# Norm factors of the memory rows: from the start of the attention to the second projection chunk

## The chip, the cores and the metric

The kernel runs on one core of a Trainium2 chip. The metric is the device time of one execution in microseconds (us). The engines are TensorE (PE, matmuls and transposes), VectorE (DVE), ScalarE (ACT), GpSimd (POOL) and SyncE (SP, which here only issues DMAs).

## The reference

One decoder layer on x of 1024 rows by 1024 columns, in float32, with 256 rows of memory. What matters here, cut:

```python
def rmsnorm(x, g):
    y = x * lax.rsqrt(jnp.mean(x * x, axis=-1, keepdims=True) + EPS)
    return y * g

def token_mixer(hn, ...):
    proj = hn @ w_in                      # split into q_a, k_a, v_a, q_i, k_i, w_i, q_b, k_b, v_b
    ...                                   # norms and rope of the heads
    out_a = dsa_attention(q_a, k_a, v_a, q_i, k_i, w_i)   # top-256 keys per query by index scores
    out_b = diff_attention(q_b, k_b, v_b, lam)            # softmax(q1 k1) - lam softmax(q2 k2), times v
    return jnp.concatenate([out_a, rms_normalize(out_b) * (1.0 - lambda_init)], axis=-1) @ w_out

def cross_attention(hn, memn, w_xq, w_xk, w_xv, w_xo, g_xq, g_xk):
    q = rmsnorm((hn @ w_xq).reshape(B, S, 4, 256), g_xq)
    k = rmsnorm((memn @ w_xk).reshape(B, 256, 4, 256), g_xk)
    v = (memn @ w_xv).reshape(B, 256, 4, 256)
    ...

h = h + token_mixer(rmsnorm(h, g_mix), ...)
h = h + cross_attention(rmsnorm(h, g_xattn), rmsnorm(mem, g_mem), ...)
h = h + conv_glu(rmsnorm(h, g_ffn), ...)
```

The change concerns `rmsnorm(mem, g_mem)`: its factor per memory row, rsqrt(mean of squares + EPS).

## The kernel before

The work runs in stages. In the first (0 to about 60 us) x is read, its rows' squares are summed, and chunk 0 of the input projection (index queries, keys and the like) is computed. Tiles of 128x1024 float32 for this lie in a ring of five buffers, pool `early`, tag "xr": raw rows of x (`xraw`) and then four `c1x` tiles, each with the results of two blocks of 128 rows. The pool is closed in chunk 1, at t == 2, and its room goes to the masks and scores of the top-k search.

Chunks 1 to 4 of the projection follow (60 to 270 us). Each has eight row tiles t: `proj_mm(c, t)` makes 24 matmuls on PE (L308 to L310, products of high and low halves), and ACT evacuates the result with the row factor (X, L646). In chunk 1 DVE, POOL, ACT and PE also work on the c1x tiles (`c1_post`, `c1_tr`: rope, splits L457/L458, key transposes L494 with their copies L496) and on index scores. In chunks 2 to 4 the threshold of the top-k search is bisected (`topk_iter`): counts by ACT (L553) for one group of row tiles and by DVE (L565) for another, with the small updates on DVE (L555, L557, L570, L571).

The differential attention starts at about 270 us, in steps s from -4. For unit u, a head and a block of 128 queries, there are: the load of the q tile `qt` (`b_load_q`, L731, SP's queue), its split on POOL into high and low part `hl` (`b_split`, L738 and L739), the transposes on PE (`b_qt`, L746, copied by ACT L748 into `qbs`), scores on PE (`b_s`, L766/L767), their masking and scaling on DVE (`e`, L774) and exponentials on ACT (L776), the difference of the two softmaxes on DVE (`b_comb`, L784 to L786), transposes of it (`b_t`, L691) and the product with v (`b_av`, L797). Keys of a head are loaded as `ktok` (L705), scaled on POOL into `kdup` (L721), transposed (L723) and split (`kb`, L725 on ACT and L726 on DVE). `b_load_v` (L712) loads `vb`.

The projections of the memory (`mem_mm`, L885, into `acc`; weights `wp` loaded at L247) are spread over the steps of this attention as units. ACT evacuates a unit with the memory rows' factors `rm` (`mem_evac`, L889); for keys a head norm follows (L894 ACT, L896, L107 to L116 and L900 DVE, with the gain product `gkq`). `mem_prep` stands ahead of the steps: it loads the two memory tiles `mtok` of 128x1024 (L873, buffers that the attention's `e` tiles use too), sums their squares on ACT (L875) into `ssm`, loads the two gains `gx` (L877, L878) and multiplies them on POOL (`gkq`, L879). At s == -2 `rstd` makes `rm` from `ssm`: ten small rows on POOL (L107, L108, L118 to L127); on DVE the same helper makes nine (L107, L108, L110 to L116).

The engines' queues are ordered by a scheduler that simulates a timeline, with the calls above as its program order. So an edit at one place can change the order of rows elsewhere.

Of the kernel before, what the change touches and what calls it, by code (L numbers as in the profile page):

```python
# [18 lines left out]
P = 128  # L19
# [25 lines left out]
def hybrid_layer(ctx, tc, I, out):  # L45
# [15 lines left out]
    def nm(s):  # L61
        cnt[0] += 1
        return f"{s}_{cnt[0]}"
# [575 lines left out]
    def proj_mm(c, t):  # L639
        pages = W.get(("in", c), 8)  # L640
        p = accp()
        s = slice(t * P, (t + 1) * P)
        for k in range(KT):
            mm3(p, xh[k][:, s], xl[k][:, s], pages[k][:, 0, :], pages[k][:, 1, :], k == 0, k == KT - 1)
        X = rt("X", [P, 512], F32, "X")
        last["act"] = act.activation(X, p, AF.Copy, scale=rx[:, t:t + 1])  # L646
        return X
# [164 lines left out]
    store = None  # L812
    idxq = [lambda t=t, h=h: idx_head(t, h) for t in range(2, NT) for h in range(4)]
    mb, sc = {}, {}
    for t in range(NT):
        X = proj_mm(1, t)
        if t == 2:
            early_st.close()
            scp_st, scp = open_pool("scp")
            for i in range(2, NT):  # L820
                mb[i] = scp.tile([P, P * (i + 1)], BF, name=f"mb{i}")
                sc[i] = scp.tile([P, P * (i + 1)], F32, name=f"sc{i}")
        if t == 7:
            W.free(8)
        W.pump(2 if t == 3 else 1)
        for a in steps[t]:
            if a == "i":
                idxq.pop(0)()
            else:
                (c1_post if a[0] == "p" else c1_tr)(int(a[1]))  # L830
        if store:
            store()
        store = proj_post(1, t, X)
# [24 lines left out]
    def etile(name):  # L858
        return obp.tile([P, T], F32, name=nm(name), tag="e", bufs=4)
# [7 lines left out]
    def mem_prep():  # L867
        pages = W.get("memT", 2)
        for j in range(KT):
            mstat[j] = pages[j // 4].bitcast(F32)[:, j % 4 // 2, (j % 2) * 256:(j % 2) * 256 + 256]  # L870
        for t in range(2):
            xt = etile("mtok")
            sp.dma_start(xt, I["mem"][t * P:(t + 1) * P, :])  # L873
            jk = rt("t2", [P, T], BF, "jk")
            act.activation(jk, xt, AF.Square, accum_out=ssm[:, t:t + 1])  # L875
        gx = rt("t2", [P, 2, 256], F32, "gx")
        sp.dma_start(gx[:, 0, :], rows(I["g_xq"]))  # L877
        sp.dma_start(gx[:, 1, :], rows(I["g_xk"]))  # L878
        pool.tensor_tensor(gkq, gx[:, 0, :], gx[:, 1, :], op=OP.mult)  # L879
# [70 lines left out]
    for s in range(-4, NB):  # L950
        h, i = b_units[max(s, 0)]
        m = s % NT

        def ok(u):
            return 0 <= u < NB
        if s % 4 == 0:
            if s >= 0:
                b_acc[s // 4] = accp()
        if s + 5 >= 2 and ok(s + 5):
            b_load_q(s + 5)  # L960
        if s >= 0 and h < 3 and m == 1:
            b_load_k(h + 1)
            b_load_v(h + 1)
        if ok(s + 4):
            b_split(s + 4)
        if s == -2:
            rstd(pool, rm, ssm, 2, 1.0 / D)
        if ok(s + 3):
            b_qt(s + 3)
        if ok(s):  # L970
            b_t(s)
        if ok(s + 2):
            b_s(s + 2)
        mem_step(MB)
        if ok(s + 1):
            b_comb(s + 1)
        if s >= 0 and h < 3 and 2 <= m <= 5:
            b_k(h + 1, (m - 2) // 2, 4 * (m % 2))
        if ok(s):
            b_av(s)  # L980
            W.pump(1)
            tick(0.8 + 0.85 * (i + 1))
# [753 lines left out]
```

## Time and profile before

| | us |
|---|---|
| median of 3 runs | 1676.73 (1675.79 to 1676.85) |
| profiled execution | 1677.18 |
| its span, first to last instruction | 1675.4 |
| PE busy / DVE / ACT / POOL | 1572.9 / 1222.3 / 804.1 / 641.2 |

Times in the trace count from the start of the span. A row of a timeline gives the start, the time and the operation with its output and input tiles (numbers left out); in brackets stands how long the engine had been idle before it, and what ended that. A row that stands for several instructions ends with their count.

### The profile page before, as it was taken

What the parts mean: (1) busy time and instruction counts of PE and PEld (TensorE: products, weight loads), DVE (VectorE), ACT (ScalarE), POOL (GpSimd) and SP (SyncE); (2) the same over time, 40 slices, a digit from 0 to 9 for tenths busy, and PEclk for the clock granted to TensorE, in tenths of its full rate; (3) what the DMA queues carried; (4) which work ended last, traced back from release to release, by engine and by line L of the source; (5) the groups of instructions that cost most, each with busy time, mean ns of one, the idle gap of its engine ahead of it and who ended that gap; (6) DMA issues with size and microseconds to landing.
All of it is one profiled execution on the core that took longest, in us unless ns stands there. A gap on an engine that the chain in (4) does not pass through costs nothing.

```text
span 1675.4 us, 22263 instructions
## 1 busy us (share of the span) xinstructions
PE 1572.9 (94%) x7596; PEld 1273.4 (76%) x7596; DVE 1222.3 (73%) x2356; ACT 804.1 (48%) x1696; POOL 641.2 (38%) x888
## 2 busy tenths in 40 slices
PE   8899987878888999999999997999999999999999
PEld 7788765666657888977777785888888777788887
DVE  5736998886778876346555369998899999865554
ACT  6545575576777445527443175432333333343432
POOL 2736656223361122031101013556666666651121
PEclk9999998989999999999999998999999999999999
DMA  8321236212120132153203021455555555799812
GB/s 283 99 83 47 77 126 212 75 51 74 49 66 27 51 101 77 45 175 115 101 1 113 26 89 63 163 170 188 177 176 178 183 187 184 253 357 379 307 51 76
DMA packets 112162, 220.06 MB, mean 131 GB/s; under 512 B 18480, under 2 KB 38448, under 8 KB 112048
## 3 DMA queue, kind: packets, MB, share of 16 engines
q1 hardware_dynamic: 91072, 148.37, 26.5%
q0 software_dynamic: 18384, 61.36, 10.3%
q10 hardware_dynamic: 2592, 8.91, 1.4%
q8 instruction: 60, 0.98, 0.2%
q14 instruction: 54, 0.44, 0.1%
HBM read 160.92 MB, written 57.67 MB: 130 GB/s over the span
## 4 chain that ended last, share of the span: by engine, by line
PE 57%; DVE 23%; DMA 7%; ACT 6%; issue 4%; POOL 3%; SPq 0%; ACTq 0%; DVEq 0%; POOLq 0%
PE acc L308 9%; PE acc L310 9%; PE acc L309 9%; PE big L309 3%; PE big L310 3%; PE big L308 3%; DVE wp L204 3%; PE acc L1036 2%; DVE jk L565 2%; PE trp L308 2%; PE trp L310 2%; PE trp L309 2%; PE trp L691 2%; DMA raw<-in_w_ffn_in_dram 2%; PE acc L885 2%
## 5 line engine op out<-in xcount | busy, mean ns | idle before, releaser
L204 DVE TENSOR_TENSOR wp<-raw,wp 128x512 fp32r<-128x512 f32 (+1 forms) x184 | 183.4, 1006 | 28.3 <-ACT wp L201 17.2
L201 ACT CAST wp<-raw 128x512 fp32r<-128x512 f32 (+1 forms) x184 | 108.4, 615 | 176.6 <-DVE raw L227 113.6
L1600 DVE TENSOR_TENSOR wp<-fo,wp 128x1024 fp32r<-128x1024 f32 x77 | 104.2, 1370 | 75.3 <-ACT wp L1599 71.6
L1549 POOL TENSOR_TENSOR fs<-fs,fs 128x512 f32<-128x512 f32 x88 | 127.6, 1450 | 63.4 <-DMA fs<-u_d 49.0
L1599 ACT CAST wp<-fo 128x1024 fp32r<-128x1024 f32 x77 | 79.8, 1049 | 107.7 <-PE big L310 46.1
L308 PE MATMUL acc<-wp,xh 128*128 128x512 f32 (+1 forms) x272 | 110.1, 407 | 10.0 <-ACT X L646 10.0
L310 PE MATMUL acc<-wp,xl 128*128 128x512 f32 (+1 forms) x272 | 109.5, 403 | 0.0
L309 PE MATMUL acc<-wp,xh 128*128 128x512 f32 (+1 forms) x272 | 109.2, 403 | 0.0
L553 ACT ACTIVATE mb<-sc,cand 128x384 bf16<-128x384 f32 (+1 forms) x96 | 75.4, 786 | 39.6 <-DVE cand L557 35.8
L203 POOL TENSOR_SCALAR wp<-raw 128x512 fp32r<-128x512 f32 (+1 forms) x36 | 24.9, 698 | 177.0 <-DVE rst L110 63.5
L682 ACT COPY pt<-trp 128x512 f32<-128x512 f32 (+3 forms) x144 | 66.3, 476 | 41.2 <-PE trp L691 40.6
L1036 PEld LDWEIGHTS acc<-va_t,pt 128*128 128x128 f32 x576 | 75.1, 196 | 9.6 <-ACT pt L682 7.6
L1036 PE MATMUL acc<-va_t,pt 128*128 128x65 f32 x576 | 77.8, 274 | 4.0 <-ACT pt L682 3.8
L1646 POOL TENSOR_TENSOR hr<-hr,r 128x512 f32<-128x512 f32 x16 | 26.8, 1686 | 115.6 <-DMA fo<-ws_d 58.4
L308 PEld LDWEIGHTS acc<-wp,xh 128*128 128x128 f32 x272 | 52.7, 194 | 23.5 <-ACT X L646 12.2
L1018 DVE CUSTOM_DVE_ANT_0 ea<-big,mb,ra 128x384 f32<-128x384 f32 (+5 forms) x48 | 45.4, 946 | 27.5 <-PE trp L691 24.4
L1497 ACT ACTIVATE fc<-fc 128x1024 f32<-128x1024 f32 x22 | 23.4, 1062 | 84.8 <-DVE fc L1496 84.8
L204 POOL TENSOR_TENSOR wp<-raw,wp 128x512 fp32r<-128x512 f32 x36 | 47.5, 1336 | 42.1 <-ACT wp L201 41.8
L774 DVE CUSTOM_DVE_ANT_0 e<-big,tri,rqk 128x1024 f32<-128x1024 f32 (+7 forms) x64 | 50.4, 812 | 16.9 <-PE big L767 14.6
L1494 ACT ACTIVATE fc<-fa,cw 128x1024 f32<-128x1024 f32 x22 | 27.4, 1245 | 71.5 <-DVE fa L1453 71.5
L1019 ACT ACTIVATE ea<-ea,sta 128x128 f32<-128x128 f32 (+7 forms) x64 | 49.5, 777 | 24.9 <-DVE sta L1018 23.0
L310 PEld LDWEIGHTS acc<-wp,xl 128*128 128x128 f32 x272 | 52.4, 193 | 11.5
(422 smaller groups left out, 5133.3 us busy)
## 6 DMA issues: line engine op xcount, KB each, us to landing
raw<-in_w_ffn_in_dram SPq DMA_DIRECT2D x44, 512.0 KB, 4.0
fs<-in_w_ffn_out_dram POOLq DMA_DIRECT2D x44, 256.0 KB, 3.5
ws_d<-fs POOLq DMA_DIRECT2D x44, 256.0 KB, 2.3
fs<-u_d POOLq DMA_DIRECT2D x44, 256.0 KB, 3.8
us_d<-fs POOLq DMA_DIRECT2D x44, 256.0 KB, 3.5
fo<-us_d SPq DMA_DIRECT2D x44, 256.0 KB, 5.4
fo<-ws_d SPq DMA_DIRECT2D x44, 256.0 KB, 5.4
u_d<-fg POOLq DMA_DIRECT2D x21, 512.0 KB, 3.7
```

The source lines that it names most:

```text
L201: act.copy(pg[:, 0, :n], src)
L204: (dve if el == "d" else pool).tensor_tensor(pg[:, 1, :n], src, pg[:, 0, :n].bitcast(F32), op=OP.subtract)
L308: pe.matmul(o, lhsT=lh, rhs=rh, start=start, stop=False)
L309: pe.matmul(o, lhsT=lh, rhs=rl, start=False, stop=False)
L310: pe.matmul(o, lhsT=ll, rhs=rh, start=False, stop=stop)
L553: act.activation(mb[i], sc[i], AF.Sign, bias=cf[:, j:j + 1], scale=-1.0, accum_out=cnt[:, j:j + 1])
L682: act.copy(dst, src)
L774: dve.tensor_tensor_reduce(e[:, :n], Ss[c][:, :n], tri[:, T - n:], rqk[h // 2][:, i, 2 * (h % 2) + c:2 * (h % 2) + c + 1], 3.0e38, OP.add, ...
L1036: pe.matmul(acc[:, hh * 65:hh * 65 + 65], lhsT=pt, rhs=va_t[:, kt, :], start=kt == 0, stop=kt == i)
L1549: pool.tensor_tensor(o, p, q, op=op)
L1599: act.copy(hi, raw)
L1600: dve.tensor_tensor(lo, raw, hi.bitcast(F32), op=OP.subtract)
```

## The change

A new function `mem_norm(t)` loads memory tile t into the ring of the first stage (tag "xr", the five buffers of 128x1024), sums its squares on ACT and, for the second tile, makes `rm` with the helper `rstd` on DVE. It is called for t = 0 and 1 right behind `proj_mm(1, t)`. The loop over the two tiles in `mem_prep` and the call of `rstd` on POOL at s == -2 are taken out.

```diff
--- before.py
+++ after.py
@@ -812,8 +812,20 @@
     store = None
     idxq = [lambda t=t, h=h: idx_head(t, h) for t in range(2, NT) for h in range(4)]
     mb, sc = {}, {}
+
+    def mem_norm(t):
+
+        xt = early.tile([P, T], F32, name=nm("mtok"), tag="xr", bufs=5)
+        sp.dma_start(xt, I["mem"][t * P:(t + 1) * P, :])
+        jk = rt("t2", [P, T], BF, "jk")
+        act.activation(jk, xt, AF.Square, accum_out=ssm[:, t:t + 1])
+        if t == 1:
+            rstd(dve, rm, ssm, 2, 1.0 / D)
+
     for t in range(NT):
         X = proj_mm(1, t)
+        if t < 2:
+            mem_norm(t)
         if t == 2:
             early_st.close()
             scp_st, scp = open_pool("scp")
@@ -868,11 +880,6 @@
         pages = W.get("memT", 2)
         for j in range(KT):
             mstat[j] = pages[j // 4].bitcast(F32)[:, j % 4 // 2, (j % 2) * 256:(j % 2) * 256 + 256]
-        for t in range(2):
-            xt = etile("mtok")
-            sp.dma_start(xt, I["mem"][t * P:(t + 1) * P, :])
-            jk = rt("t2", [P, T], BF, "jk")
-            act.activation(jk, xt, AF.Square, accum_out=ssm[:, t:t + 1])
         gx = rt("t2", [P, 2, 256], F32, "gx")
         sp.dma_start(gx[:, 0, :], rows(I["g_xq"]))
         sp.dma_start(gx[:, 1, :], rows(I["g_xk"]))
@@ -963,8 +970,6 @@
             b_load_v(h + 1)
         if ok(s + 4):
             b_split(s + 4)
-        if s == -2:
-            rstd(pool, rm, ssm, 2, 1.0 / D)
         if ok(s + 3):
             b_qt(s + 3)
         if ok(s):
```

On POOL, at the start of the attention, this stood before (`rst` and `rm` are the norm factors, `hl` with `qt` the split of a q tile, `kdup` scaled keys, `gkq` the gain product):

```order
L122 TENSOR_TENSOR rst_2762<-rst_2762 128x2
L123 TENSOR_TENSOR rst_2762<-rst_2762 128x2
L738 TENSOR_SCALAR hl_2759<-qt_2744 128x2x64
L124 TENSOR_SCALAR rst_2762<-rst_2762 128x2
L739 TENSOR_TENSOR hl_2759<-qt_2744,hl_2759 128x2x64
L125 TENSOR_TENSOR rst_2762<-rst_2762 128x2
L126 TENSOR_SCALAR rst_2762<-rst_2762 128x2
L127 TENSOR_TENSOR rm<-rst_2762 128x2
L738 TENSOR_SCALAR hl_2801<-qt_2757 128x2x64
L739 TENSOR_TENSOR hl_2801<-qt_2757,hl_2801 128x2x64
L721 TENSOR_TENSOR kdup_3016<-ktok_2894,rqk_76 128x4x64 x2
L879 TENSOR_TENSOR gkq<-gx_2737 128x256
```

And this stands there now, right behind the same splits of the first two q tiles:

```order
L886 TENSOR_TENSOR gkq<-gx_2747 128x256
L738 TENSOR_SCALAR hl_2769<-qt_2754 128x2x64
L721 TENSOR_TENSOR kdup_3013<-ktok_2891,rqk_76 128x4x64 x2
L739 TENSOR_TENSOR hl_2769<-qt_2754,hl_2769 128x2x64
L738 TENSOR_SCALAR hl_2798<-qt_2767 128x2x64
L721 TENSOR_TENSOR kdup_3081<-ktok_2892,rqk_76 128x4x64 x2
L721 TENSOR_TENSOR kdup_3138<-ktok_2891,rqk_76 128x4x64 x2
L739 TENSOR_TENSOR hl_2798<-qt_2767,hl_2798 128x2x64
```

The norm factors are gone; the gain product has come ahead of the third q tile's split, and two rows of scaled keys between its halves L738 and L739.

On SP's queue at the same place, the loads before (`wp` weights of the memory projection, `vb` values, `qa_d` a store of normed queries of the other attention):

```order
L247 DMA wp_3157<-in_w_xv_dram 128x2x512
L712 DMA vb_2727<-vb_d 128x8x128
L873 DMA mtok_2729<-in_mem_dram 128x1024
L873 DMA mtok_2733<-in_mem_dram 128x1024
L712 DMA vb_2902<-vb_d 128x8x128
L247 DMA wp_3211<-in_w_xv_dram 128x2x512
L675 DMA qa_d<-X_2599 128x512
L731 DMA qt_2744<-qk_d_91 128x128
L705 DMA ktok_2894<-qk_d_91 128x4x128
L675 DMA qa_d<-X_2654 128x512
L731 DMA qt_2757<-qk_d_91 128x128
```

And the loads now:

```order
L247 DMA wp_3154<-in_w_xv_dram 128x2x512
L712 DMA vb_2745<-vb_d 128x8x128
L712 DMA vb_2899<-vb_d 128x8x128
L247 DMA wp_3208<-in_w_xv_dram 128x2x512
L675 DMA qa_d<-X_2617 128x512
L884 DMA gx_2747<-in_g_xq_dram 128x256
L885 DMA gx_2747<-in_g_xk_dram 128x256
L731 DMA qt_2754<-qk_d_91 128x128
L705 DMA ktok_2891<-qk_d_91 128x4x128
L675 DMA qa_d<-X_2672 128x512
L731 DMA qt_2767<-qk_d_91 128x128
```

Two loads of 128x1024 are gone, and the two gain loads have moved from behind the keys to the place ahead of the first q tile.

On DVE in chunk 1 of the projection the rows of the norm factors (`rst`, nine rows, the last into `rm`) now stand between the rope of c1x tiles; the rows without `rst` and `rm` stood there before in the same order:

```order
L452 TENSOR_TENSOR c1x_548<-c1x_548,tb_785 128x64
L107 TENSOR_SCALAR rst_849<-ssm 128x2
L481 TENSOR_TENSOR c1x_548<-c1x_548,t_128_788 128x384
L108 TENSOR_SCALAR rst_849<-rst_849 128x2
L483 TENSOR_SCALAR kk_123_764<-c1x_548,rka 128x128
L452 TENSOR_TENSOR c1x_553<-c1x_553,csn 128x320
L110 SCALAR_TENSOR_TENSOR rst_849<-rst_849 128x2
L497 TENSOR_TENSOR ka_102<-trp_668,ka_101 128x128
L452 TENSOR_TENSOR c1x_553<-c1x_553,tb_867 128x64
L111 TENSOR_TENSOR rst_849<-rst_849 128x2
L481 TENSOR_TENSOR c1x_553<-c1x_553,t_143_870 128x384
L112 SCALAR_TENSOR_TENSOR rst_849<-rst_849 128x2
```

So the first row of `rst`, which waits for ACT's second square, stands ahead of one c1x tile's L481 and of its key scaling L483.

## Rows read from the trace of the kernel before

**Rows 1.** The page's first part: busy time, share of the span, instructions.

```profile
PE 1572.9 (94%) x7596; PEld 1273.4 (76%) x7596; DVE 1222.3 (73%) x2356; ACT 804.1 (48%) x1696; POOL 641.2 (38%) x888
```

**Rows 2.** Windows: us, busy time and instructions by engine, granted PE clock, DMA share, GB/s.

```profile
70.00:190.00 120.00, 120.00 (x548) 97.94 (x547) 74.24 (x146) 61.34 (x122) 68.87 (x104) 1.00 0.23 72
280.00:290.00 10.00, 3.78 (x14) 2.63 (x12) 6.08 (x16) 5.81 (x13) 2.38 (x7) 0.71 1.07 339
310.00:320.00 10.00, 6.04 (x39) 5.14 (x38) 10.00 (x24) 6.54 (x16) 2.41 (x4) 0.92 0.26 84
```

**Rows 3.** Waits, 262 to 312 us: who waited for whom, us in total, times, longest.

```profile
POOL rst L107 <- ACT jk L875: 7.7, 1, 7.7
PE trp L746 <- POOL hl L739: 7.6, 1, 7.6
```

**Rows 4.** Chain of work that ended last, 250 to 312 us: start, us, what.

```profile
273.93 9.68 DMA mtok<-in_mem_dram
```

**Rows 5.** Timeline of SP's DMA queue: start, us of the issue, line, transfer.

```profile
282.06 0.38 SPq L731 DMA_DIRECT2D qt<-qk_d  x1
```

**Rows 6.** DMA issues at 282.0 to 282.4 us: size, us from issue to landing.

```profile
qt<-qk_d SPq DMA_DIRECT2D x1, 64.0 KB, 7.3
```

**Rows 7.** Timeline of POOL, 269 to 302 us: start, us, operation, tiles, idle time before.

```profile
287.10 0.19 POOL L107 TENSOR_SCALAR rst<-ssm 128x2 f32<-128x2 f32 x1 [7.70 <-ACT jk L875]
...
290.21 0.30 POOL L738 TENSOR_SCALAR hl<-qt 128x128 fp32r<-128x128 f32 x1
...
290.90 0.46 POOL L739 TENSOR_TENSOR hl<-qt,hl 128x128 fp32r<-128x128 f32 x1
...
292.83 1.20 POOL L721 TENSOR_TENSOR kdup<-ktok,rqk 128x256 f32<-128x256 f32 x2
293.99 0.73 POOL L879 TENSOR_TENSOR gkq<-gx 128x256 f32<-128x256 f32 x1
```

**Rows 8.** Timeline of DVE, 269 to 302 us.

```profile
284.87 0.48 DVE L774 CUSTOM_DVE_ANT_0 e<-big,tri,rqk 128x256 f32<-128x256 f32 x1 [0.72 <-ACT jk L875]
...
288.17 0.17 DVE L784 RECIPROCAL st<-st 128x2 f32<-128x2 f32 x1 [2.40 <-ACT e L776]
...
293.62 0.69 DVE L896 TENSOR_REDUCE ss<-sq 128x2 f32<-128x512 f32 x1 [0.72 <-ACT sq L894]
...
295.30 0.56 DVE L111 TENSOR_TENSOR rst<-rst 128x2 f32<-128x2 f32 x1
...
297.53 1.14 DVE L774 CUSTOM_DVE_ANT_0 e<-big,tri,rqk 128x896 f32<-128x896 f32 x1
```

**Rows 9.** Timeline of PE, 269 to 320 us.

```profile
291.42 0.69 PE L746 MATMUL trp<-ident,hl 128*128 128x128 f32 x2 [7.64 <-POOL hl L739]
...
294.12 0.78 PE L766 MATMUL big<-kb,qbs 128*128 128x512 f32 x1
...
312.56 0.50 PE L766 MATMUL big<-kb,qbs 128*128 128x512 f32 x1 [2.03 <-DVE st L774]
...
317.90 0.33 PE L691 MATMUL trp<-ident,e 128*128 128x128 f32 x1 [1.93 <-DVE kb L726]
```

**Rows 10.** Timeline of ACT, 269 to 302 us.

```profile
283.69 1.06 ACT L875 ACTIVATE jk<-mtok 128x1024 bf16<-128x1024 f32 x1 [3.17 <-DMA mtok<-in_mem_dram]
```

**Rows 11.** Timeline of ACT, 44 to 80 us.

```profile
61.20 0.41 ACT L457 CAST hl<-c1x 128x256 fp32r<-128x256 f32 x1 [2.76 <-DVE hl L458]
...
65.38 0.27 ACT L496 CAST ka<-trp 128x128 fp32r<-128x128 f32 x1 [2.99 <-PE trp L494]
...
73.01 0.69 ACT L646 ACTIVATE X<-acc,rx 128x512 f32<-128x512 f32 x1 [2.00 <-PE acc L310]
```

**Rows 12.** DMA issues at 50.7 to 50.9 us.

```profile
raw<-in_w_in_dram SPq DMA_DIRECT2D x1, 512.0 KB, 4.7
```

**Rows 13.** Waits, 190 to 242 us.

```profile
PE acc L308 <- ACT X L646: 10.0, 5, 3.9
```

**Rows 14.** The page's costliest groups: xcount | busy, mean ns | idle before.

```profile
L553 ACT ACTIVATE mb<-sc,cand 128x384 bf16<-128x384 f32 (+1 forms) x96 | 75.4, 786 | 39.6 <-DVE cand L557 35.8
```

## The prediction

> **What bounds the kernel now.** I read the page first. TensorE (PE) works for 1572.9 us, 94% of a span of 1675.4 us [rows 1], so a change off PE can only win where PE stands still. The windows by stage say where that is: from 70 to 190 us PE is busy all the time [rows 2], while in 280 to 290 us it works 3.78 us of 10 and VectorE (DVE) 6.08. That second place is the start of the differential attention, which the change touches.
>
> The list of waits of 262 to 312 us says who waits there [rows 3]: PE waits 7.6 us, once, for POOL's row L739 (the split of a q tile); POOL itself waits 7.7 us, once, for ScalarE's (ACT's) square L875 of a memory tile. The chain of waits goes one step further back, in one row: 9.68 us of "DMA mtok", the tile's load [rows 4]. So the program looks as if it stood still for memory rows that nobody needs yet, with the q tile queued behind the norm factors on POOL.
>
> Three more views are needed before that 7.6 us may be believed. First the DMA issues: the q tile `qt` that L738/L739 split is issued on SP's queue at 282.06 [rows 5] and takes 7.3 us to land [rows 6]. It lands at 282.06 + 7.3 = 289.4 us. POOL's wait ends at 287.10, and L738 runs at 290.21 [rows 7]: without any norm factors, POOL could have started the split only 0.8 us earlier. The load takes 7.3 us because the DMA engines are full: share 1.07 and 339 GB/s in 280 to 290 us [rows 2].
>
> Second, DVE. It waits 2.40 us for ACT's exponentials at 288.17, 0.72 us for an ACT square at 284.87 and 0.72 us for an ACT square of the memory keys at 293.62 [rows 8]. The next score rows `e` (step 2) start on DVE at 297.53 only, although PE's matmuls for them began at 294.12 [rows 8, 9].
>
> Third, what ends last behind this. In 310 to 320 us DVE is busy for the whole 10 us and PE for 6.04 [rows 2]; PE waits there 2.03 us for DVE's statistics (L774) and 1.93 us for DVE's `kb` (L726) [rows 9]. So what the start of the attention is worth is set by how early DVE gets through its own rows, and PE can give up at most these waits plus what it gains itself.
>
> **The change, part by part.** All times below are from the one profiled execution.
>
> *Removed: two memory loads.* 2 x 512 KB = 1.05 MB leave the queue ahead of the q tile. At 339 GB/s this is 1.05 MB / 339 GB/s = 3.1 us for all that lands behind them. The order of SP's queue shows that the two gain loads `gx` (2 x 128 KB = 0.26 MB, 0.8 us at the same rate) now stand ahead of the q tile, where before they stood behind it. So the q tile should land at 289.4 - 3.1 + 0.8 = 287.1 us, and `ktok` right behind it, whose 256 KB take 0.8 us at that rate, at 287.9 us.
>
> *Removed: ten POOL rows of norm factors.* On POOL now stand ahead of L739: `gkq` (0.73 us), L738 (0.30) and two `kdup` rows (1.20 together) [rows 7]. From 286.9 us, when `gx` should be there: gkq to 287.6, L738 to 287.9, kdup to 289.1, L739 (0.46) to about 289.6. PE's transposes of this tile began at 291.42 [rows 9]; they should begin at about 289.7. **PE's own gain is 1.7 us**, not 7.6, since most of the wait goes from POOL's square to POOL's data.
>
> *Removed: two ACT squares from the place.* Each is 1.06 us [rows 10] and the reading of its sum behind it; together over 2.1 us that stood among the exponentials. They are why DVE waited 2.40 and 0.72 us [rows 8]. The evacuation of the first memory unit (L889) no longer waits for `rm`, so the key norm on DVE (L896, L107 to L116) can run while DVE had nothing to do; the order shows these rows ahead of and between the first score rows. **DVE's gain is at most 0.72 + 2.40 + 0.72 = 3.84 us.** Step 2's score matmuls stood 2.7 us behind the transposes, since the cast between them waited behind L889 on ACT; without that they start at about 290.8 rather than 294.12, 3.3 us earlier, and so don't hold DVE back from taking its 3.84.
>
> Which of 1.7 and 3.84 counts? PE's two waits for DVE at 312.56 and 317.90 [rows 9] are the next thing that ends last, so it is nearer to DVE's. I go seven tenths of the way from the one to the other: 1.7 + 0.7 x 2.14 = 3.2 us, with 1.7 and 3.84 as the bounds.
>
> *Added in the first stage: two loads, two squares, nine DVE rows.* The squares come on ACT behind rows at which ACT stood idle (2.99 us before 65.38, 2.00 us before 73.01 [rows 11]): two of 1.06 us fit. The first load stands ahead of one weight load that took 4.7 us [rows 12]; 512 KB more at 339 GB/s makes that 1.5 us later. ACT, which casts these weights, then had 2.76 us idle before 61.20 [rows 11], which takes it in. The second load takes the slot of a c1x tile and can start only when DVE and ACT have read that; I put this at 66.5 us, and at 4.7 us it lands by 71.2, when ACT has just become free (73.01 - 2.00 = 71.0). The nine DVE rows cost at most 0.56 us each by a row of the same helper on as few columns [rows 8], so 5.0 us; DVE works 74.24 of 120 us in 70 to 190 us while PE is full [rows 2]. The cover for all this is PE's projection matmuls. If it is gone, because the second load comes later than 71.8 us, the X evacuation at 73.01 and the transposes behind DVE come late by as much: up to 2 us. I take 0.
>
> *Moved: the rows between 195 and 270 us.* The scheduler orders each queue anew. At five places an X evacuation (L646) now stands behind one more pair of top-k counts (L553) on ACT. PE waits there for just these evacuations: 10.0 us in 5 waits [rows 13]. But DVE, which releases these counts, has up to 2 us less work ahead of them in the new order (and the nine norm rows lie earlier, in idle time). I take 0, with -1.5 and +2 as bounds.
>
> *Moved: the rows of the attention itself,* up to about 470 us. The same work in another order; I take 0, and 2 us to either side.
>
> **Sum.** 0 + 0 - 3.2 = -3.2 us. The profiled execution took 1677.18 us with a span of 1675.4; it should become 1674.0 with a span of 1672.2. It lies 0.45 us above the median of the runs, 1676.73, so the prediction is 1673.5 us. A difference of 0.2% (3.35 us) is about what a measurement of this kernel tells from no change.
>
> **The rivals.**
>
> *A: the whole wait goes.* If the q tile is not held up by what stands ahead of it, POOL is through with it as soon as PE asks, and the 7.6 us of [rows 3] vanish: 1676.73 - 7.6 = 1669.1 us. For it speaks that the profile names ACT's square as releaser; against it the 7.3 us from issue to landing of a load of 64 KB [rows 6]. The Trainium skill, page "DMA: Bandwidth & Descriptors", section "Anatomy of one DMA — SWDGE (gpsimd) path", puts a DMA at a fixed 2.0 us plus its bytes at 436 GB/s, which for 64 KB gives an estimate of 2.15 us and a landing at about 284.2 us; by that rule the load would be ready long before POOL and this rival would hold. The trace does not agree with it here (7.3 us), since the rule is one for a DMA by itself.
>
> *B: nothing is left of it.* DVE's rows from 301 us on are the chain anyway, and the freed 3.84 us are spent on waits in another order (POOL's kdup waits for `ktok` with the q tile's L739 behind it). For it speaks DVE's 10.00 of 10 us in 310 to 320 us and that the memory units move too. It decides if DVE's new waits exceed 3 us. Time: about 1676.5 us.
>
> *C: slower, by the evacuations in 195 to 240 us.* A pair of counts on ACT is 2 x 786 ns = 1.6 us [rows 14]. If DVE isn't earlier by the 2 us that I read from the order, five evacuations are each 1.6 us later where PE already waits: +8.0 - 3.2 = +4.8 us, 1681.5 us. Two late ones cancel the gain, four make it slower by 3.2 us, and with the fifth it is slower by more than 0.2%.
>
> **How the numbers follow.** The forecast has 0.43, with its own range 1671.8 to 1675.2; it lies astride the bound for faster, so 0.22 of it is faster and 0.21 the same. A has 0.20, all faster. B has 0.20, all the same. C has 0.17, of which 0.14 slower and 0.03 the same. Faster: 0.42; same: 0.44; slower: 0.14. The range runs from just below A, 1668.8, to 1679.0, which takes in C's smaller half and the bounds of +2 us and leaves out C's tail.
>
> **What would show it.** In the changed profile: no "POOL rst L107" wait; PE's stall before the third L746 begins at about the same time and still lasts 5 to 6.5 us, released by POOL's L739; the q tile lands at about 287; POOL waits there for a DMA (gx or ktok). `e` of step 2 on DVE at about 293.5 rather than 297.53, `kb` L726 some 3 us earlier than 317.18. Up to 195 us PE's rows are as before to within 0.5 us, and the sum of its waits for L646 stays within 2 us of 10.0. I am wrong if that sum grows by over 3 us, if PE's stall falls below 3 us (A), or if the offset that is gained at 300 us is gone again by 470 us.

## The result and the profile after

The changed kernel takes 1667.53 us (median of 7 runs, 1664.02 to 1671.46); the kernel before, beside it on the same chip, 1676.73 us (7 runs, 1675.26 to 1678.81). The ratio is 0.9945 with the interval 0.9929 to 0.9960: 9.2 us faster. 1673.5 us was predicted, with a range from 1668.8 to 1679.0 us, so the time lies 1.3 us below the range and 6 us below the forecast. The profiled execution took 1669.67 us with a span of 1667.9 us. PE's work is the same; less time lies between it. In the page's first part, PE's busy time is 2.5 us less than in [rows 1], and the span 7.5 us less:

```profile
PE 1570.4 (94%) x7596; PEld 1268.6 (76%) x7596; DVE 1214.7 (73%) x2365; ACT 804.8 (48%) x1696; POOL 638.4 (38%) x876
```

The waits from 262 to 312 us, against [rows 3]: who waited for whom, us in total, times, longest.

```profile
POOL gkq L886 <- DMA gx<-in_g_xk_dram: 8.2, 1, 8.2
...
PE trp L746 <- POOL hl L739: 7.4, 2, 6.4
```

POOL's wait for ACT's square (7.7 us) has gone, and in its place stands one for the gain loads `gx`, of 8.2 us (6.8 us in a second profile). PE's wait for the split q tile went from 7.64 to 6.39 us. The DMA issues and POOL's timeline say why, first the two gain loads and then the q tile with size and us from issue to landing:

```profile
gx<-in_g_xq_dram SPq DMA_DIRECT2D x1, 128.0 KB, 5.2
gx<-in_g_xk_dram SPq DMA_DIRECT2D x1, 128.0 KB, 5.5
...
qt<-qk_d SPq DMA_DIRECT2D x1, 64.0 KB, 4.0
```

SP's queue and POOL's timeline around them:

```profile
285.59 0.38 SPq L731 DMA_DIRECT2D qt<-qk_d  x1
```

```profile
289.51 0.72 POOL L886 TENSOR_TENSOR gkq<-gx 128x256 f32<-128x256 f32 x1 [8.22 <-DMA gx<-in_g_xk_dram]
290.20 0.30 POOL L738 TENSOR_SCALAR hl<-qt 128x128 fp32r<-128x128 f32 x1
290.48 1.52 POOL L721 TENSOR_TENSOR kdup<-ktok,rqk 128x256 f32<-128x256 f32 x2
291.96 0.45 POOL L739 TENSOR_TENSOR hl<-qt,hl 128x128 fp32r<-128x128 f32 x1
```

The q tile's load is 3.3 us faster than in [rows 6], where two loads of 512 KB went ahead of it on the queue, but in this profile it is issued at 285.59 us and not at 282.06 [rows 5], and so lands at 289.6. In a second profile of the changed kernel (an experiment below) it is issued at 282.40, takes 5.2 us and lands at 287.6; the weight load ahead of it holds SP's queue for 5 us in both. The four POOL rows are just those that the prediction had put ahead of PE's transposes.

PE, DVE and ACT, against [rows 8, 9, 11]; first PE, with one score matmul from before the stall for comparison:

```profile
281.85 0.39 PE L767 MATMUL big<-kb,qbs 128*128 128x512 f32 x1
...
292.47 0.69 PE L746 MATMUL trp<-ident,hl 128*128 128x128 f32 x2 [6.39 <-POOL hl L739]
293.68 0.80 PE L766 MATMUL big<-kb,qbs 128*128 128x512 f32 x1 [0.52 <-ACT qbs L748]
294.27 0.63 PE L767 MATMUL big<-kb,qbs 128*128 128x512 f32 x1
...
315.88 0.33 PE L691 MATMUL trp<-ident,e 128*128 128x128 f32 x1 [0.82 <-DVE kb L726]
```

DVE, the first score row of step 2:

```profile
295.57 1.15 DVE L774 CUSTOM_DVE_ANT_0 e<-big,tri,rqk 128x896 f32<-128x896 f32 x1 [1.03 <-PE big L767]
```

ACT in the second projection chunk, with the two moved squares:

```profile
63.06 1.05 ACT L821 ACTIVATE jk<-mtok 128x1024 bf16<-128x1024 f32 x1
...
72.09 1.06 ACT L821 ACTIVATE jk<-mtok 128x1024 bf16<-128x1024 f32 x1
...
74.19 0.69 ACT L646 ACTIVATE X<-acc,rx 128x512 f32<-128x512 f32 x1 [0.95 <-PE acc L310]
```

The squares lie where ACT was idle: its wait before the evacuation at 74.19 is 0.95 us, against 2.00 us at 73.01 in [rows 11]. So PE was not kept waiting. The 1.2 us between the two starts of that evacuation are not the moved work's: at 43 us, ahead of it, the offset is 1.4 us already.

**Where the time went.** To see it, each profile's rows are laid against those of the first profile of before: the start of the same row (same line, same count) in the one less that in the other is an offset, and its growth from one point to the next is what a stage gains or loses. The points are ACT's 16th and last X evacuation (161.7 and 269.7 us in before) and DVE's score rows `e` L774 number 9, 21, 33 and 64 (311.5, 345.7, 385.6, 465.6 us), then the first L1497 (1056 us) and the last L1600 (1656 us). At ACT's third X evacuation (73 us) and at the first point the offset of each profile is the same to 0.1 us; in the two profiles of the changed kernel it is 1.2 and 1.4 us. Between the two, single evacuations lie up to 1 us off that, and in the extra rows' kernel up to 3 us. Such a constant comes from the program's start (the three profiles of before have 0, -1.2 and 1.3), so where single times are compared below it is taken off. Changes in us, negative is a gain:

| kernel | 162-270 | 270-311 | 311-346 | 346-386 | 386-466 | 466-1056 | 1056-1656 |
|---|---|---|---|---|---|---|---|
| before, second profile | 1.0 | -0.5 | -1.2 | -0.1 | 0.0 | -1.1 | 2.9 |
| before, third profile | 1.2 | 0.4 | -1.2 | -3.0 | -1.2 | -0.4 | 1.9 |
| changed | 2.0 | -4.9 | -1.1 | -5.1 | -1.2 | 0.7 | 1.0 |
| changed, second profile | 0.8 | -5.3 | -1.1 | -4.5 | -0.8 | -0.9 | 4.2 |
| norm in both places | 1.9 | -3.4 | -1.8 | -4.5 | -0.8 | -0.8 | 18.1 |
| no norm | -0.2 | -4.5 | -0.7 | -4.9 | -0.9 | 0.5 | 1.0 |
| norm on POOL | -0.3 | -2.7 | -1.1 | -5.1 | -1.3 | -2.4 | 2.4 |
| extra rows | -1.4 | -0.8 | -1.1 | 0.0 | -0.1 | -4.2 | 3.5 |
| one edge | 0.2 | -1.6 | -0.8 | -3.9 | 2.1 | -4.6 | 2.6 |
| one edge, second profile | 1.1 | 0.2 | -0.5 | -4.3 | 2.1 | -4.9 | -0.3 |
| gains early | 0.8 | -5.0 | -2.0 | -4.8 | 1.5 | -2.6 | 0.8 |
| gains early, second profile | 2.1 | -6.0 | -1.6 | -4.9 | -1.0 | -0.8 | 0.3 |
| norm on POOL and gains early | 1.1 | -6.1 | 0.6 | -4.9 | 0.5 | -1.2 | 16.8 |

In the one edge's two rows the point of 465.6 us misleads: that kernel's order puts this very score row 2.4 and 2.7 us later. By score row number 63, just ahead of it, its growth from 386 us on is -0.3 and -0.6, and from there to 1056 us -2.3 and -2.2.

The two further profiles of before say how far such a number may be read: the same queues, stage by stage, differ by up to 3 us (the third profile at 346 to 386 us). In the changed kernel two stages stand out from that. One is the start of the attention, where the gain was predicted. The other, 346 to 386 us, lies 50 us behind every row that the change edits, and there nothing was predicted.

What PE waits for there; the kernel before, and then the changed kernel:

```profile
351.18 1.16 PE L797 MATMUL acc<-vb,pt 128*128 128x128 f32 x8 [3.15 <-ACT pt L682]
...
370.59 1.54 PE L691 MATMUL trp<-ident,e 128*128 128x128 f32 x6 [3.34 <-DVE kb L726]
```

```profile
345.96 1.16 PE L797 MATMUL acc<-vb,pt 128*128 128x128 f32 x8 [0.46 <-ACT pt L682]
...
364.35 0.66 PE L691 MATMUL trp<-ident,e 128*128 128x128 f32 x4 [0.73 <-ACT qbs L748]
```

Both kernels have the same work there; the scheduler put it in another order. ACT ahead of the first of these waits, before:

```profile
348.24 1.04 ACT L776 ACTIVATE e<-e,st 128x896 f32<-128x896 f32 x1 [0.20 <-DVE st L774]
...
349.53 1.03 ACT L553 ACTIVATE mb<-sc,cand 128x896 bf16<-128x896 f32 x1
...
350.56 1.05 ACT L682 COPY pt<-trp 128x512 f32<-128x512 f32 x2
```

And changed:

```profile
345.33 1.06 ACT L682 COPY pt<-trp 128x512 f32<-128x512 f32 x2
346.27 1.06 ACT L776 ACTIVATE e<-e,st 128x896 f32<-128x896 f32 x1
...
347.31 1.04 ACT L553 ACTIVATE mb<-sc,cand 128x896 bf16<-128x896 f32 x1
```

Before, the two `pt` copies for which PE waits stand behind an exponential (1.04 us) and a top-k count (1.03 us); in the changed kernel they stand ahead of both. PE's wait shrinks from 3.15 to 0.46 us.

The windows of this stage show a second part of it. Columns as in [rows 2]; before, and then the changed kernel's windows 6 us earlier, which hold the same work:

```profile
346.00:356.00 10.00, 6.32 (x43) 5.75 (x42) 9.52 (x32) 7.38 (x19) 0.87 (x3) 0.83 0.23 67
356.00:366.00 10.00, 7.88 (x55) 6.62 (x54) 8.06 (x25) 8.40 (x22) 2.64 (x6) 1.00 0.04 13
366.00:376.00 10.00, 6.66 (x34) 6.33 (x33) 9.90 (x32) 6.82 (x17) 3.08 (x6) 0.68 0.31 88
376.00:386.00 10.00, 10.00 (x37) 5.67 (x37) 1.75 (x6) 2.89 (x7) 3.55 (x5) 0.98 0.36 111
```

```profile
340.00:350.00 10.00, 7.30 (x54) 6.56 (x55) 8.80 (x32) 8.99 (x25) 1.82 (x5) 1.00 0.37 100
350.00:360.00 10.00, 7.38 (x51) 5.98 (x50) 9.89 (x34) 8.32 (x21) 2.67 (x6) 1.00 0.04 13
360.00:370.00 10.00, 8.45 (x43) 6.61 (x42) 9.68 (x27) 8.41 (x20) 3.04 (x6) 0.83 0.32 88
370.00:380.00 10.00, 9.73 (x46) 6.25 (x46) 4.68 (x17) 3.84 (x9) 4.73 (x7) 1.00 0.38 118
```

The granted clock (the number behind the bracketed counts) is 0.83 and 0.68 in the two windows that hold the 3.15 and 3.34 us waits; in the changed kernel one window is at 0.83 and the others at full clock (in its second profile another one of the four). A granted clock below 1 is time at the lower of the two levels, 1.2 instead of 2.4 GHz. If PE had work for all of such a time, ten microseconds at a clock of c lose (1 - c) x 10. That is 1.7 + 3.2 + 0.2 = 5.1 us before and 1.7 us after, an upper bound since PE also stood idle for part of it. So some of the gain may be not in PE's wait rows at all, but in the matmuls behind them.

### The profile page after: what moved, and what is told of

Read it like the earlier page. It is cut to its first block, busy times and chain, and to the rows that moved or that the text cites. A ratio compares the mean times of both kernels' runs of the same rounds, so it can differ in the third digit from the quotient of the medians.

```text
span 1667.9 us, 22267 instructions
## 1 busy us (share of the span) xinstructions
PE 1570.4 (94%) x7596; PEld 1268.6 (76%) x7596; DVE 1214.7 (73%) x2365; ACT 804.8 (48%) x1696; POOL 638.4 (38%) x876
## 4 chain that ended last, share of the span: by engine, by line
PE 64%; DVE 20%; DMA 6%; ACT 4%; issue 3%; POOL 3%; ACTq 0%; SPq 0%; POOLq 0%; DVEq 0%
PE acc L308 10%; PE acc L310 10%; PE acc L309 10%; PE big L309 4%; PE big L310 4%; PE big L308 4%; DVE jk L565 3%; PE trp L310 3%; PE trp L309 3%; PE trp L308 3%; PE acc L1041 2%; PE trp L691 2%; PE big L1280 2%; PE acc L892 2%; DVE wp L204 2%
## 5 line engine op out<-in xcount | busy, mean ns | idle before, releaser
L308 PEld LDWEIGHTS acc<-wp,xh 128*128 128x128 f32 x272 | 52.5, 193 | 22.4 <-ACT X L646 11.2
L309 PEld LDWEIGHTS acc<-wp,xh 128*128 128x128 f32 x272 | 52.5, 193 | 14.0 <-POOL wp L204 2.7
```

What stands on the lines that cost most here:

```text
L308: pe.matmul(o, lhsT=lh, rhs=rh, start=start, stop=False)
L309: pe.matmul(o, lhsT=lh, rhs=rl, start=False, stop=False)
```

## The experiments

Theory at the start: of the 9 us, about 4 come from the start of the attention as predicted, and the rest from the order in which the scheduler puts the untouched attention rows (346 to 386 us above all). Rivals: the removed POOL wait is worth the whole; or moving the norm costs and gains in other stages. Each timed kernel was timed beside the kernel before.

**The norm in both places.** The kernel before, with the new code added into tiles `rm2`, `ssm2` that nothing reads; the old norm, with its wait, stays.

```
+    def mem_norm(t):
+        xt = early.tile([P, T], F32, name=nm("mtok"), tag="xr", bufs=5)
...
+        act.activation(jk, xt, AF.Square, accum_out=ssm2[:, t:t + 1])
+        if t == 1:
+            rstd(dve, rm2, ssm2, 2, 1.0 / D)
...
+        if t < 2:
+            mem_norm(t)
```

> The new early norm runs as in the changed kernel, but into factors that nothing reads; the old loads, squares and POOL rows at the start of the attention stay and make the factors that are used. Theory P (three places: the new order of chunks 2 to 4 costs about 2 us, the start of the attention wins about 5, the new order of the attention's later steps wins about 7): this kernel has the changed kernel's order in chunks 2 to 4 and in the later steps, and the old start, so 1676.7 + 2 - 7 = about 1672 us; PE's wait for L739 stays near 7.6 us. Rival W (all of the gain is the wait that was removed at the start): nothing is won, 1676 to 1679 us.

1682.3 us (7 runs, 1681.89 to 1686.31), ratio 1.0048 (1.0030 to 1.0066): slower. Its waits from 262 to 312 us still have the old chain, and DVE still waits for ACT's squares and for the exponentials among them (line numbers are higher here: L748, L741, L109 and L888 are L746, L739, L107 and L875 of before, and L776, L778 and L786 are L774, L776 and L784):

```profile
PE trp L748 <- POOL hl L741: 8.0, 2, 7.0
POOL rst L109 <- ACT jk L888: 7.3, 1, 7.3
```

```profile
285.52 0.48 DVE L776 CUSTOM_DVE_ANT_0 e<-big,tri,rqk 128x256 f32<-128x256 f32 x1 [0.72 <-ACT jk L888]
...
288.82 0.17 DVE L786 RECIPROCAL st<-st 128x2 f32<-128x2 f32 x1 [2.40 <-ACT e L778]
...
295.20 1.14 DVE L776 CUSTOM_DVE_ANT_0 e<-big,tri,rqk 128x896 f32<-128x896 f32 x1
```

And yet, up to 466 us, the table shows it 8.6 us faster than before, against 10.3 and 10.9 for the changed kernel: -3.4 at the start, where the wait still stands, and -4.5 at 346 to 386 us. By this one profile the wait that the change takes away is worth about 2 us, and the new order of the rows the rest; 2 us is no more than two profiles of the same queues differ. The time is lost again behind 1056 us (+18.1), in the feed-forward stage, where this kernel's queues have another order than those of before and of the changed kernel. What that loss is, a later experiment asks.

**No norm at all.** The changed kernel without `mem_norm`, so that the factors are not computed: `rm` is set to 1.

```
+    dve.memset(rm, 1.0)
     for t in range(NT):
...
-        if t < 2:
-            mem_norm(t)
```

> The norm of the memory rows is left out: no loads, no squares, the factors are set to 1 at the beginning. The order of chunks 2 to 4 is that of the kernel before, the order of the attention that of the changed kernel. Theory P: -5 - 7 = 1664.7 us, some 2 to 3 us under the changed kernel. Rival W: as the changed kernel, 1667.5 us. If neither the start nor the later steps matter: 1676 us.

1669.76 us (12 runs, 1665.86 to 1679.03), ratio 0.9965 (0.9949 to 0.9982). By the ratio it is no faster than the changed kernel: the moved norm costs nothing that these runs can tell in the chunk where it now stands. POOL's wait for `gx` is there too (7.2 us), and PE's for the q tile is 6.1 us: they don't need the norm.

**The norm's ten rows on POOL,** but in the second chunk, as the scheduler puts them once the squares are early.

```
-        if t == 1:
-            rstd(dve, rm, ssm, 2, 1.0 / D)
...
+        if s == -2:
+            rstd(pool, rm, ssm, 2, 1.0 / D)
```

> Loads and squares of the memory rows in chunk 1 as in the changed kernel, but the ten small rows of the factors on POOL (the order puts them in chunk 1 as well). DVE gets no new rows there, and chunks 2 to 4 keep the order of the kernel before; the attention has the order of the changed kernel. Theory P: as without any norm, 1664.7 us, 2 to 3 us under the changed kernel, with PE's waits for L646 in 195 to 240 us as before (10.0 us). Rival W: 1667.5 us. If the squares or loads in chunk 1 cost something, it is above the kernel without a norm by that.

1670.85 us (12 runs, 1665.21 to 1675.34), ratio 0.9968 (0.9953 to 0.9984). By the ratio it is the changed kernel again, so which engine computes the factors makes no difference that these runs can tell. What this kernel, the one without a norm and the changed kernel share is that no loads and squares of the memory rows stand at the start of the attention, and the new order of the attention.

**Extra rows that nothing reads.** The kernel before with nine small DVE rows more in the second chunk and no other edit: it leaves the old norm and its wait.

```
+        if t == 1:
+            rstd(dve, rm2, ssx[:, 0:2], 2, 1.0 / D)
```

> The kernel before with nine more small DVE rows in chunk 1, on factors that nothing reads. The order of chunks 2 to 4 changes (in another way than in the changed kernel), the order of the attention does not. Theory P: only the projections can differ, 1676.7 plus or minus 3 us, and the offset against the kernel before is constant from 270 us on. Rival S (any edit that shuffles the queues is worth several us by luck, the content does not matter): a difference of more than 4 us to either side.

1669.34 us (11 runs, 1665.18 to 1676.22), ratio 0.9962 (0.9943 to 0.9981): nearly as much gained as by the change, by rows that add work. They change the order in the projection chunks and, in the attention, that of some DVE, ACT and PE rows between 303 and 334 us. Behind that the order is that of before; accordingly the table has 0.0 at 346 to 386 us. Its profile gains 4.1 us from the first point to the end, but no stage of the differential attention stands out (-0.8 and -1.1 us up to 346 us, where a repeat of before has -0.5 and -1.2; -1.4 in the projections, -4.2 from 466 to 1056 us, +3.5 behind). Where its gain comes from stays open. It is the strongest warning here: a reshuffle alone moves this kernel by 6.2 us in the median (from 1675.49 us), close to the size of the result.

**One ordering edge.** The kernel before, with one count in the step of 346 us held behind the `pt` copies by an explicit order; no instruction is added or taken away. The scheduler then also puts other rows in another order, mostly of DVE and ACT, from 349 to 379 us and from 446 to 476 us by the times of the kernel before, and a few later on: it is one edge, but more than one moved row.

```
-                with tc.issue_after(last["act"].ins), tc.issue_after(last["dve"].ins):
+                with tc.issue_after(last["act"].ins), tc.issue_after(last["dve"].ins), tc.issue_after(last[pin[0]].ins):
...
-        act.copy(dst, src)
+        last["pt"] = act.copy(dst, src)
...
+            pin[0] = "pt" if s == 8 else "act"
             tick(0.8 + 0.85 * (i + 1))
+            pin[0] = "act"
```

> The kernel before with one ordering edge: the top-k rows that are issued at the end of attention step 8 have to stand behind the copies L682 of that step's transposes. The norm stays at its old place, with its wait. By the order this moves one count on ACT behind two copies and a few DVE rows of the next steps, at 350 to 372 us. Theory P2 (most of the change's gain is the order of these rows, 5.2 us between the unit scores at 346 and at 386 us of the kernel before): the offset against the kernel before goes from about 0 at 346 us to -3 to -5 at 386 us and stays; 1670 to 1673 us on the chip of before's 1675.5 to 1676.7. Rival W (the removed wait): no difference.

> The kernel with one ordering edge again. If its step of -3.9 us between 346 and 386 us in the first profile is that of its order, it has it again, against each profile of the kernel before; if it was scatter, it is near 0 here or in the further profiles of the kernel before.

In both of its profiles the stage is 3.9 and 4.3 us shorter, and PE's two waits of 3.15 and 3.34 us shrink (line numbers are one higher here); the first profile:

```profile
348.35 1.16 PE L798 MATMUL acc<-vb,pt 128*128 128x128 f32 x8 [0.53 <-ACT pt L683]
...
365.73 0.88 PE L692 MATMUL trp<-ident,e 128*128 128x128 f32 x6 [1.90 <-DVE kb L727]
```

The profiled executions took 1671.47 and 1669.96 us, 5 to 7 us less than those of before (1677.18, 1676.99 and 1676.1). But its timed runs have a median of 1676.33 us (12 runs, 1669.19 to 1681.87), ratio 1.0001 (0.9980 to 1.0022). So in its profiles the edge does in the stage what the theory says, and the median of its runs does not show it; the two profiles lie in the fast part of its own runs. That contradiction was not resolved.

**The gain loads early.** The changed kernel, with the two `gx` loads and their product moved to the third step of the second chunk, so that POOL has nothing ahead of the q tile.

```
+            gkq = scp.tile([P, 256], F32, name="gkq")
+            gx = rt("t2", [P, 2, 256], F32, "gx")
+            sp.dma_start(gx[:, 0, :], rows(I["g_xq"]))
+            sp.dma_start(gx[:, 1, :], rows(I["g_xk"]))
+            pool.tensor_tensor(gkq, gx[:, 0, :], gx[:, 1, :], op=OP.mult)
...
-    gkq = obp.tile([P, 256], F32, name="gkq")
...
-        gx = rt("t2", [P, 2, 256], F32, "gx")
-        sp.dma_start(gx[:, 0, :], rows(I["g_xq"]))
-        sp.dma_start(gx[:, 1, :], rows(I["g_xk"]))
-        pool.tensor_tensor(gkq, gx[:, 0, :], gx[:, 1, :], op=OP.mult)
```

> The changed kernel, with the two gain loads and their product on POOL moved into chunk 1, so that POOL waits for neither norm nor gains at the start of the attention. If PE's wait there is for the q tile's data: POOL's wait of 8.2 us for the gains becomes one for the q tile of about 7 us, PE's wait for L739 falls from 6.4 us to some 4 to 5 (gains and two rows of scaled keys out of the way), the time is 1 to 2 us under the changed kernel. If the wait was for whatever stood ahead on POOL: PE's wait vanishes, 1661 to 1662 us.

> The sixth experiment once more, beside the eleventh on one chip. If its lead over the changed kernel is real: 1664 to 1668 us, ratio 0.993 to 0.996 to the kernel before. If the sixth's was scatter: 1668 to 1672 us. In its profile TensorE's stall before the q tile's transposes should again be under 3 us with the wait for the q tile's own data on POOL.

1666.44 us (12 runs, 1663.97 to 1671.18), ratio 0.9944 (0.9925 to 0.9962), and on another chip 1667.48 us (5 runs), ratio 0.9944 (0.9925 to 0.9964). POOL now waits for the q tile itself, and PE's stall of 6.39 us becomes two short ones (first profile):

```profile
285.34 0.30 POOL L738 TENSOR_SCALAR hl<-qt 128x128 fp32r<-128x128 f32 x1 [6.45 <-DMA qt<-qk_d]
```

```profile
286.27 0.69 PE L746 MATMUL trp<-ident,hl 128*128 128x128 f32 x2 [2.60 <-POOL hl L739]
289.43 0.69 PE L746 MATMUL trp<-ident,hl 128*128 128x128 f32 x2 [2.47 <-DVE st L785]
```

With norm and gains out of the way POOL still waits 6.45 us, for a load: behind the wait for the norm stood one for data. PE's first stall is 3.8 us shorter, but the second takes 2.47 us of that back, and the stage gains 0.4 us (the means of -5.0 and -6.0 against -4.9 and -5.3): the second stall is one for DVE's statistics, and DVE's rows end last there, as the prediction had it. This is the fastest kernel measured, but its ratio is that of the changed kernel's first measurement (0.9945), so a lead of its own is not shown.

**The changed kernel once more,** on the chip of the one edge's and the early gains' first timing.

> The changed kernel again, on the chip of these runs. Theory P2: 1667.5 us and a ratio near 0.9945; its offset against the kernel before at 346 us is -3, at 386 us -8, as in its first profile, since the queues are the same.

1669.82 us (12 runs, 1665.01 to 1675.93) beside 1676.97 us, ratio 0.9964 (0.9946 to 0.9982): 7.2 us gained where the first measurement had 9.2. The intervals overlap.

**The kernel before, twice more,** a profile each, to see how far two profiles of the same queues differ.

> The kernel before, a second profiled execution: how far do two executions of the same queues differ by stage? If the stages are as fixed as their queues, all offsets against the first profile lie within 1 us, and the steps of -5 us (270 to 298 us) and -5 us (346 to 386 us) that kernels with the changed order show against it are real. If this execution differs by several us in these stages, a part of them is scatter, and the granted clock will show it (8.6 us of full-speed time lost to the low clock in 270 to 330 us and 8.5 in 330 to 480 us in the first profile).

> The kernel before, a third profiled execution, for the scatter of its stages: the two readings are those written for the second one (within 1 us of the first profile in every stage, or several us apart with the low clock to show for it).

1676.99 and 1676.1 us. The second profile repeats the first at 346 to 386 us (-0.1, waits of 3.13 and 3.33 us). The third gains 3.0 us there with the old order:

```profile
352.94 1.16 PE L797 MATMUL acc<-vb,pt 128*128 128x128 f32 x8 [1.64 <-ACT pt L682]
...
371.94 0.90 PE L691 MATMUL trp<-ident,e 128*128 128x128 f32 x6 [1.89 <-DVE kb L726]
```

So the old order does not always cost the whole 5 us. The means of this stage over the three profiles of before and the two of the changed kernel are -1.0 and -4.8 us: the order is worth 3.8 us there, within a scatter of the old order of 0 to 3.

**The norm on POOL and the gains early,** the third and the sixth edit together. Its feed-forward queues have the order that the first experiment had, but the norm is computed once.

> The changed kernel with the ten norm-factor rows on POOL (still in the second projection chunk, as in the third experiment) and the gain loads early (as in the sixth). Its feed-forward stage has the queue order that the first experiment had there, and it computes the norm once. Theory (the first experiment lost its time by that feed-forward order): as early as the sixth by the end of attention (-9 to -11 us of offset), then 16 to 18 us lost between 1056 us and the end, 1680 to 1684 us in all. Rival (it lost it by computing the norm twice, which isn't done here): 1664 to 1668 us, with no growth of the offset after 1056 us.

1679.24 us (10 runs, 1675.44 to 1683.69), ratio 1.0012 (0.9996 to 1.0029); the profiled execution, 1683.69 us, is the slowest of the ten. Up to 466 us it is as far ahead as the others (-8.8 from the first point), and behind 1056 us it loses 16.8 us. That takes the double computation out as the reason of the first experiment's loss: what the two share is the order of the feed-forward queues, which from 1056 us on is the same on every engine. In the median of its runs it is 2.6 us slower than before, a little less than the 1680 us that the theory gave as its least. PE's waits from 1050 to 1500 us (DVE's L1458 is L1453 of before):

```profile
PE big L308 <- DVE fa L1458: 3.8, 4, 1.4
PE acc L308 <- DVE fa L1458: 3.6, 4, 1.5
PE acc L308 <- DVE fg L1458: 3.1, 1, 3.1
PE trp L308 <- DVE fa L1458: 2.5, 3, 1.1
```

They and three more sum to 15.6 us; in the kernel before all waits of this list in that stretch are 3.8 us. This is 11.8 us more, where the offset grows by 10.5 us up to 1449 us. Which of POOL's and SP's swapped rows makes DVE late was not tried.

## Why the prediction was wrong, point by point

**The first stage: 0, right.** The offset is the same at 73 and at 162 us, and leaving the norm out gains nothing that can be told.

**The moved projection rows: 0 between -1.5 and +2, right, on its high side.** 162 to 270 us has +1.4 as the mean of the two changed profiles and +0.7 over the three of before, so +0.7. Rival C, which has PE's waits for the evacuations grow, fell; they did not grow:

```profile
PE acc L308 <- ACT X L646: 9.0, 5, 5.7
```

against 10.0 in 5 waits [rows 13].

**The start of the attention: -3.2, too small by 1 to 2 us, and near in size only in part for the reasons given.** Measured from 270 to 311 us: -5.1 against 0.0; with the 0.7 lost just ahead of it, -4.4, where 0 - 3.2 stood. Rival A fell: PE's stall stays (6.39 us; 5.8 in the second profile), and its cause is data, first `gx` and behind that the q tile. The single times agree to about 1 us once the start-up constant is taken off, for the first and the second profile: the q tile lands at 288.4 and 286.2 us (287.1 forecast), the score rows of step 2 start on DVE at 294.4 and 293.1 (293.5 forecast), and PE's first transpose behind `kb` is 3.2 and 4.8 us earlier than in [rows 9] (3 forecast). PE's own share was forecast too large: its transposes begin at 291.3 and 290.0 us, 0.1 and 1.4 us earlier and not 1.7. In the first profile the reason is mostly that `gx` lands late: `gkq` starts at 288.3 us and not at 286.9. In the second it is the two `kdup` rows ahead of L739, 2.16 us and not 1.20 [rows 7]. The score matmuls start at 292.5 and 291.2 us, where 290.8 stood, and in the first profile DVE does wait for them (1.03 us), which the forecast had left out. The prediction put their lateness in the kernel before down to a cast on ACT; PE's own rows stood there too, two transposes L746 and four L691 from 292.93 to 294.47 us.

The gain comes through DVE, as the prediction said, but only in part as the three waits that it counted. The norm in both places keeps the waits of 0.72 and 2.40 us, and still, counted from 270 us, its first score row of step 2 starts 4.7 us earlier than before, against 5.1 and 5.3 in the changed kernel. What differs there is the order: in the kernel before, the key norm's rows L107 to L114 stand ahead of that score row on DVE, from 294.65 us on; in the norm in both places it stands ahead of them. By the table the removed waits are then worth 1.5 to 1.9 us of this stage (-4.9 and -5.3 against -3.4), by one profile of that kernel. So that 3.2 came near 4.4 is in part luck.

By the rule of the Trainium skill that rival A named (page "DMA: Bandwidth & Descriptors", section "Anatomy of one DMA — SWDGE (gpsimd) path") the q tile's load takes an estimated 2.15 us; the trace has 7.3 before, 4.0 and 5.2 after, and so agrees in none. The prediction's reason for that, that the rule is one for a DMA by itself, is not shown: the section is on DMAs that GpSimd issues, this load is issued on SP's queue, and no run here separates the two.

**The moved attention rows: 0 with 2 us to either side. This is the step that failed.** The prediction put it as "The same work in another order; I take 0, and 2 us to either side". Measured from 311 to 466 us, in the means of two profiles against three: -0.3 - 3.8 - 0.6 = -4.7 us, 3.8 of them at 346 to 386 us. That the order does it in this stage is shown by both profiles of the one edge (-3.9 and -4.3), and by the eight profiles with the new order (-4.5 to -5.1) against 0 (the first of before, by definition), -0.1, -3.0 and 0.0 with the old; that it adds up in the total is not, since the timed runs of the one edge don't show it. The stage could have been read beforehand: the trace of before has its 3.15 and 3.34 us waits, and the new order takes the `pt` copies from behind 2 us of ACT rows. The prediction looked for waits up to 320 us and no further. How far the total missed depends on the timing: the second, 1669.82 us, would lie inside the range, though its gain of 7.2 us is still more than twice the forecast.

**A price that was left out: the clock behind a stall.** Waits were priced one for one. From windows over 270 to 330, 330 to 390 and 390 to 480 us, with (1 - clock) x length, the granted clock is 0.86, 0.91 and 0.96 before and 0.91, 0.97 and 0.98 in the changed kernel's first profile. Before loses up to 60 x 0.14 + 60 x 0.09 + 90 x 0.04 = 17.4 us at the lower level, its further profiles 15.6 and 12.0 (mean 15.0); the changed kernel 9.0 and 10.8 (mean 9.9). Up to 5 us of the gain can lie in these matmuls. How much of that is on the path was not separated from the waits themselves, and it is contained in the stage numbers above, not to be added to them.

The sum of all stages, means against means, is +0.7 - 5.1 - 0.3 - 3.8 - 0.6 + 0.4 + 1.0 = -7.7 us (the last two from 466 to 1056 and to 1656 us). The timed differences are 9.2 and 7.2 us. What the prediction gave as the sign of its being wrong, that the gain of 300 us is gone again by 470, did not come: the gain doubled.

**What stays open:** why extra rows that nothing reads gain 0.4% without the new attention order, and why one edge gains in its profiles and not in its timed runs. Both say that some 5 us of this kernel's time can hang on the order of its queues and on scatter (29 runs of the kernel before on one chip lie between 1669.27 and 1687.08 us), and that a single cause for the whole 9.2 us isn't established.

## What to carry to other kernels

When a scheduler orders the queues anew, cost the change over the whole reach in which the orders differ, not only around the edited lines: go through the trace of before for waits of the bounding engine, and look in the new order for what now stands ahead of each row it waits for. Before a few microseconds of one stage are put down to a cause, profile the unchanged kernel a second and third time, and time one kernel that only reshuffles; here that alone gave 0.4%. And when a wait seems to be for a computation, ask when the data behind it lands and when its issue comes: of the 7.6 us that seemed to hang on the norm, 6.4 were still there without it.

## What the runs showed of the hardware

A stall in PE's row can cost more than its own time. Behind the 6.39 us stall that ends at 292.47 us a 128x512 score matmul shows 0.63 us, where the same matmul at 281.85 shows 0.39 us; the transposes behind the 2.60 and 2.47 us stalls of the early gains show 0.69 us as well, so splitting one stall into two did not spare it. Not every stall shows it: behind the 2.03 us stall that ends at 312.56 us in the kernel before [rows 9], the next score matmul of that size, at 312.89, shows 0.40 us. That these are rows at the lower level, 1.2 instead of 2.4 GHz, is read from the granted clock of such places: 0.71 in before's window of 280 to 290 us [rows 2], 0.83 and 0.68 at the two waits above. The Trainium skill, page "TensorE: Matmul & The Clock Gate", section "What's actually happening", has just these two levels; the windows' fractions are then mixtures of both within ten microseconds. What this can cost varies between executions: two profiles with the same queues, the first and the third of before, differ by 5.4 us in what they can lose at the lower level between 270 and 480 us (17.4 and 12.0, by the sums above), though their whole times differ by only 1.1 us.
